# Experts' second half: conversions two half chunks ahead, sums behind the next quarter's first half chunk, the last group's work spread out

## The chip, the cores and the metric

The kernel runs on one core of a Trainium2 chip. The metric is the device time of one execution in microseconds (us), the median of several runs. The engines are TensorE (PE, with its weight loads PEld), VectorE (DVE), ScalarE (ACT), GpSimd (POOL) and SyncE (SP), whose queue here only issues DMAs. PE writes its results into eight PSUM banks of 128 x 512 fp32.

## What is computed

One layer for 512 tokens of width 2048: a mixer (pooling, retention, gates, an output projection) and behind it a PEER layer of 16384 experts. The change lies in the experts' second half and the end of the kernel. Cut to that, the reference is:

```
def block(args):                       # the experts, for 128 tokens
    xb, eb, gb = args                  # tokens, chosen experts, gates
    u = expert_u[eb]
    v = expert_v[eb]
    act = jax.nn.gelu(jnp.einsum('td,tkd->tk', xb, u))
    return jnp.einsum('tk,tkd->td', gb * act, v)
...
x = x + g2[:, None, :] * peer_ffn(fn, ...)
return rmsnorm(x, final_norm_gain)
```

## The kernel before, in words

Every fp32 product is made of three TensorE products: each operand is split into a high part (fp32r) and a low part, and `mm3` (lines 83 to 87) adds high x high, high x low and low x high. So each operand has to be converted: `split` (lines 71 to 74) has ACT write the high part (L73) and DVE the low part (L74).

**The first three blocks of 128 tokens** (`acc0` to `acc2`) are multiplied densely with all experts, **the fourth block** (`accg`) gathers its 128 chosen rows of `v` one after another: POOL issues an indirect DMA into one of three buffers `vrow` (L928), DVE multiplies the row by its coefficient and adds it to `accg` (L1078).

`experts_out` (L1052) runs over 16 groups of 8 x 128 experts. A group has four quarters of 512 output columns, and a quarter has four half chunks, so a group has 16 half chunks (the number `step` in the code, 0 to 15). A half chunk is 128 x 1024 values of `v`: two experts' 512 columns. For each, PE does 2 experts x 3 token blocks x 3 products = 18 matmuls (288 in a group), into three PSUM banks that the whole quarter adds up. `pairs` are the converted activations `ph` and `pl` that stand against it, eight per group.

What feeds PE in a group, in the order of the code:

- `half()` (L143) hands out a converted half chunk and then converts until `converted` of them are ready, here 1. A conversion takes 128 x 1024 of a 1 MB chunk `rawc` and writes `whc` (ACT) and `wlc` (DVE). There are three `whc`/`wlc` pairs and three `rawc` buffers; once both halves of a chunk are converted, `fill` issues the DMA for the third chunk after it on SP's queue. Half chunk s + 1 is thus converted in program order ahead of the matmuls of half chunk s.
- Behind the matmuls of half chunks 0, 1, 2, 4, 5, 6, 8, 10 and 12 one gathered row is added (L1078), until all 128 are done, which is early in the 15th group.
- At half chunk 4 `load_group` (L1032) issues the next group's gates `gt` and activations `at` on SP. At half chunks 9, 10, 11 and 13 `gate_in` has POOL multiply two of them by their gates (L1049), and `halves` has ACT and DVE convert them into `ph` and `pl`.
- At the end of a quarter DVE adds the three banks to `acc` (L1187). These sums stand in DVE's queue right behind the quarter's last half chunk, so DVE waits there until PE has finished it, and the conversion of the next quarter's second half chunk is queued behind them.

All engines work through their queues in program order (this part of the program is scheduled by hand).

**The last group** also ends the layer. `close(q)`, behind the second half chunk of a quarter, has POOL multiply that quarter of the four results by the row g2 (L1111), PE transpose the residual (L1115) and DVE add it (L1118). `finish` (L1121) multiplies the last banks by g2 (L1124), adds them (L1125) and has ACT sum the squares (L1105). The rows g2 and the final gain are loaded at the start of the stage, on ACT's queue (L1062, L1063). The last quarter goes block by block: its four half chunks are converted first (a fourth pair lies in `vrow`), then `close(3)` and `put` of the gathered block, then for each block 24 matmuls, `finish` and `put`. `put` (L1132) computes the inverse root mean square and scales two halves of 1024 columns: for three of the four tiles with two DVE instructions that multiply by the gain as well (L1139), for the last block with one on ACT (L1143) and one on DVE (L1141), after `gained` (L1130) has multiplied by the gain quarter by quarter, three times on POOL and in the last quarter on DVE.

## Time and profile before

| | us |
|---|---|
| median of 3 runs (5053.54 to 5059.59) | 5055.97 |
| the profiled execution's own time | 5052.76 |
| its span, first to last instruction | 5051.0 |
| PE busy in the span | 4850.2 (96%) |
| DVE / ACT / POOL busy in the span | 3240.8 / 1704.6 / 1504.5 |
| the experts' second half, from its first to its last matmul | 3890.04 to 5031.9 |

The profile is that of one execution. A busy share says little by itself here; what counts is where PE waits. The views used are: busy time per engine in stretches of time (with the granted clock of TensorE and the DMA engines' busy share), the list of who waited for whom, groups of instructions by line, and the instructions in order of time. Start times are from the start of the span. In an instruction's row the bracket says how long its engine stood idle before it and what ended that. Matmul ends are modelled: a matmul of 512 columns is drawn as 0.39 us but the next one starts about 0.227 us after it.

### The profile page before, as it was taken

The page shows a single profiled execution, that of the slowest core. Times are in us where ns is not written, and L with a number is a line of the kernel's source. Part 1 is how long each engine was busy: PE and PEld are TensorE (multiplying, and loading weights), DVE is VectorE, ACT ScalarE, POOL GpSimd, SP SyncE. Part 2 cuts the span into 40 slices and gives each one's busy share as a digit, 9 for nine tenths or more (in the row PEclk, how much of TensorE's full clock was granted, in tenths as well). Part 3 has the DMA queues.
Part 4 walks back from the last instruction along what each step waited for, and adds up shares of the span by engine and source line. Part 5 has one row for each costly group of instructions (what it writes and reads, how often), then busy time and mean ns, then how long its engine had stood idle before and what let it go on. Part 6 is the DMA issues. An engine that isn't in the chain of part 4 may idle for free.

```text
span 5051.0 us, 58652 instructions
## 1 busy us (share of the span) xinstructions
PE 4850.2 (96%) x22905; PEld 4181.8 (83%) x22905; DVE 3240.8 (64%) x4297; ACT 1704.6 (34%) x2700; POOL 1504.5 (30%) x1115
## 2 busy tenths in 40 slices
PE   6889999999999999999999999999999999999997
PEld 5668888888888888888778999999999777777776
DVE  8873333443432245565477998888786787887876
ACT  3232222222232222122232365556564322222222
POOL 6440000000000011000011478779685333333322
PEclk9999999999999999999999999999999999999999
DMA  6442233222233356665623688878888888888873
GB/s 261 177 144 94 94 102 102 94 100 101 93 135 122 123 215 241 233 243 204 214 91 107 222 285 296 300 273 304 307 303 315 292 312 302 289 298 296 308 250 134
DMA packets 268022, 1058.12 MB, mean 209 GB/s; under 512 B 22608, under 2 KB 73856, under 8 KB 172768
## 3 DMA queue, kind: packets, MB, share of 16 engines
q1 hardware_dynamic: 208240, 724.62, 41.6%
q0 software_dynamic: 54416, 325.48, 17.0%
q10 hardware_dynamic: 5088, 4.26, 0.3%
q8 instruction: 181, 2.97, 0.2%
q14 instruction: 97, 0.79, 0.0%
HBM read 973.53 MB, written 80.75 MB: 209 GB/s over the span
## 4 chain that ended last, share of the span: by engine, by line
PE 63%; DVE 14%; DMA 9%; issue 9%; POOL 2%; ACT 2%; SPq 1%; POOLq 0%; DVEq 0%; ACTq 0%
PE bank L86 21%; PE bank L87 20%; PE bank L85 20%; DMA at<-ga 4%; DVE wlc L74 3%; DMA rawc<-in_w_ada_dram 2%; DVE urow L977 2%; DMA gd<-gsc 1%; DVE rawc L187 1%; DMA rawc<-in_v_dram 1%; DVE accg L1078 1%; ACT whc L73 1%; DVE pl L74 1%; POOL ohx L917 1%; PE bank L906 1%
## 5 line engine op out<-in xcount | busy, mean ns | idle before, releaser
L74 DVE TENSOR_TENSOR wlc<-rawc,whc 128x1024 fp32r<-128x1024 f32 x904 | 1205.3, 1335 | 1018.3 <-ACT whc L73 1017.4
L73 ACT CAST whc<-rawc 128x1024 fp32r<-128x1024 f32 x967 | 999.5, 1050 | 2011.3 <-PE bank L86 1084.3
L85 PE MATMUL bank<-act,whc 128*128 128x512 f32 x2816 | 1102.5, 392 | 27.7 <-ACT act L346 19.8
L86 PE MATMUL bank<-act,whc 128*128 128x512 f32 x2816 | 1103.1, 392 | 23.6 <-DVE act L355 18.8
L87 PE MATMUL bank<-act,wlc 128*128 128x512 f32 x2816 | 1102.3, 391 | 6.7 <-POOL wlc L74 5.1
L87 PE MATMUL bank<-fh,wlc 128*128 128x384 f32 (+1 forms) x2304 | 791.9, 344 | 10.1 <-DVE wlc L74 8.9
L85 PE MATMUL bank<-fh,whc 128*128 128x384 f32 (+1 forms) x2304 | 793.0, 344 | 3.1 <-ACT fh L730 2.0
L86 PE MATMUL bank<-fl,whc 128*128 128x384 f32 (+1 forms) x2304 | 790.9, 343 | 0.6 <-DVE fl L733 0.5
L86 PE MATMUL bank<-wlc,ph 128*128 128x512 f32 x1530 | 607.5, 397 | 55.2 <-DVE wlc L74 55.2
L86 PEld LDWEIGHTS bank<-act,whc 128*128 128x128 f32 x2816 | 531.8, 189 | 140.5 <-DVE act L355 23.1
L85 PEld LDWEIGHTS bank<-act,whc 128*128 128x128 f32 x2816 | 532.2, 189 | 139.9 <-ACT act L346 19.8
L87 PEld LDWEIGHTS bank<-act,wlc 128*128 128x128 f32 x2816 | 531.9, 189 | 120.2 <-POOL wlc L74 6.6
L917 POOL TENSOR_SCALAR ohx<-iota,tr,gh 128x128 fp32r<-128x128 f32 x384 | 595.2, 1556 | 76.7 <-PE bank L906 72.6
L85 PE MATMUL bank<-whc,ph 128*128 128x512 f32 x1530 | 603.5, 394 | 4.6 <-ACT whc L73 3.1
L87 PE MATMUL bank<-whc,pl 128*128 128x512 f32 x1530 | 602.9, 394 | 0.0
L87 PEld LDWEIGHTS bank<-fh,wlc 128*128 128x128 f32 x2304 | 435.8, 189 | 22.5 <-DVE wlc L74 10.2
L85 PEld LDWEIGHTS bank<-fh,whc 128*128 128x128 f32 x2304 | 436.7, 190 | 13.4 <-ACT fh L730 2.3
L86 PEld LDWEIGHTS bank<-fl,whc 128*128 128x128 f32 x2304 | 436.0, 189 | 11.3 <-DVE fl L733 1.9
L86 PEld LDWEIGHTS bank<-wlc,ph 128*128 128x128 f32 x1530 | 291.7, 191 | 129.6 <-DVE wlc L74 69.4
L928 POOL DMA_INDIRECT vrow<-in_v_dram,eidx x128 | 222.5, 1738 | 519.6 <-DVE accg L1078 505.6
L187 DVE SCALAR_TENSOR_TENSOR rawc<-rawc,cond 128x2048 f32<-128x2048 f32 x96 | 239.8, 2498 | 182.3 <-DMA rawc<-in_w_ada_dram 182.2
L85 PEld LDWEIGHTS bank<-whc,ph 128*128 128x128 f32 x1530 | 291.6, 191 | 68.8 <-ACT whc L73 5.2
(289 smaller groups left out, 5236.4 us busy)
## 6 DMA issues: line engine op xcount, KB each, us to landing
rawc<-in_ut_dram SPq DMA_DIRECT2D x128, 1024.0 KB
rawc<-in_v_dram SPq DMA_DIRECT2D x128, 1024.0 KB
rawc<-in_w_ada_dram SPq DMA_DIRECT2D x96, 1024.0 KB
rawc<-in_w_v_dram SPq DMA_DIRECT2D x32, 1024.0 KB
rawc<-in_w_g_dram SPq DMA_DIRECT2D x32, 1024.0 KB
rawc<-in_w_br_dram SPq DMA_DIRECT2D x32, 1024.0 KB
ga<-gao SPq DMA_DIRECT2D x64, 384.0 KB
gd<-gsc SPq DMA_DIRECT2D x24, 1024.0 KB
```

The source lines that it names most:

```text
L73: nc.scalar.copy(out=h, in_=src)
L74: (eng or nc.vector).tensor_tensor(out=l, in0=src, in1=h.bitcast(FT), op=OP.subtract)
L85: mm(out, w[0], x[0], start=start, stop=False)
L86: mm(out, w[0], x[1], start=False, stop=False)
L87: mm(out, w[1], x[0], start=False, stop=stop)
L187: nc.vector.scalar_tensor_tensor(out=t, in0=t, scalar=1.0, in1=self.cond, op0=OP.mult, op1=OP.mult, accum_out=self.mod[:, j:j + 1])
L906: nc.tensor.matmul(bank[:, u * 2 * P:(u + 1) * 2 * P], y, x.rearrange("p h i -> p (h i)"), start=True, stop=True)
L917: nc.gpsimd.tensor_scalar(out=x[:, 0, :], in0=self.iota, scalar1=tr[:, 0, s], scalar2=gh[:, s].bitcast(FT), op0=OP.is_equal, op1=OP.mult)
L928: self.nc.gpsimd.indirect_dma_start(out=t, out_offset=None, in_=src, in_offset=bass.IndirectOffsetOnAxis(ap=self.eidx[:, k:k + 1], axis=0))
L977: nc.vector.scalar_tensor_tensor(out=u, in0=u, scalar=1.0, in1=fnat, op0=OP.mult, op1=OP.mult, accum_out=act[:, i:i + 1])
L1078: stt(out=accg, in0=v, scalar=c, in1=accg, op0=OP.mult, op1=OP.add)
```

## The change

In the 16 groups:

- `converted` becomes 2 and two more pairs (`w5`) are set up, five in all (`cycle` 5: three from the old buffers, two from the new). Half chunk s + 2 is now converted, in program order, ahead of the matmuls of half chunk s.
- The three sums of a quarter (`add_up`) move behind the first half chunk of the next quarter in the code, and so behind one more conversion.

In the last group and its neighbour:

- g2 and the gain are no longer loaded at the start of the stage. In the 15th group, at half chunk 13, SP issues the residual's first three parts, then g2 into the free `gt` buffer and the gain into the four free `at` buffers.
- `close` is split: `gate(q)` (POOL times g2) comes at half chunk 15 of the 15th group and at 2, 5, 8 of the last, `residual(q)` (transposes and additions) at 1, 4, 7, 10.
- `gained` is called for all four tiles and all quarters: 13 times on POOL, 3 times (last quarter) on DVE. `put` therefore scales each tile with one ACT and one DVE instruction.
- The conversions for the last quarter start at half chunks 10 and 11 (`converted` 3 and 4), all through the five pairs; `spare` goes. `put` of the gathered block comes before the last quarter's loop over blocks.

```diff
-        if self.extra_pair and self.pairs_made % 4 == 3:
+        if self.extra_pair and self.pairs_made % self.cycle >= 3:
             return self.extra_pair()
...
-            pp, ac, vp = tp("pp", 2), tp("ac"), tp("vp", 3)
+            pp, ac, vp, more = tp("pp", 2), tp("ac"), tp("vp", 3), tp("w5", 2)
+            self.extra_pair, self.cycle, self.converted = lambda: self.pair_of(more), 5, 2
...
-            nc.scalar.dma_start(out=g2, in_=self.g2row.to_broadcast([P, D]))
-            nc.scalar.dma_start(out=gain, in_=a["final_row"].to_broadcast([P, D]))
...
+            def load_lines():
+                g = self.gl.tile([P, ND // GC, G, GC], FT, name="gt").rearrange("p a b c -> p (a b c)")[:, :D]
+                nc.sync.dma_start(out=g, in_=self.g2row.to_broadcast([P, D]))
+                for q in range(4):
+                    w = self.ld.tile([P, 2, ND], FT, name="at").rearrange("p a b -> p (a b)")[:, :T]
+                    nc.sync.dma_start(out=w, in_=a["final_row"][:, cut(q)].to_broadcast([P, T]))
+                    lines[q] = g[:, cut(q)], w
...
+            def add_up(g, q, banks):
+                for t in range(NT):
+                    o = acc[t][:, cut(q)]
+                    if g == 0:
+                        nc.scalar.copy(out=o, in_=banks[t])
+                    else:
+                        tt(out=o, in0=o, in1=banks[t], op=OP.add)
...
+                    if last and step >= 10:
+                        self.converted = step - 7
+                    w = self.half()
+                    if hf == 0:
+                        banks = [self.bank() for _ in range(NT)]
...
+                    if full:
+                        add_up(*full)
+                        full = None
...
+                    if g == NGR - 2:
+                        if step == 13:
...
+                            for i in range(3):
+                                load(i)
+                            load_lines()
+                        if step == 15:
+                            gate(0)
+                    if last:
+                        if step in (2, 5, 8):
+                            gate(step // 3 + 1)
+                        if step in (1, 4, 7, 10):
+                            residual(step // 3)
...
+                            full = g, q, banks
...
             ws = [self.half() for _ in range(4)]
+            put(NT)
             for t in range(NT):
...
                 finish(t, 3, b)
                 put(t)
```

Three places where instructions stand in another order. The first is DVE's queue in the third quarter of a middle group: `wlc` is a conversion, `pl` the low part of an activation of the next group, `accg` a gathered row, `acc` a sum. Before, from the conversion of half chunk 10 to the first sum:

```order
L74 TENSOR_TENSOR wlc<-rawc,whc 128x1024
L74 TENSOR_TENSOR pl_32420<-at,ph_32419 128x384
L74 TENSOR_TENSOR pl_32424<-at,ph_32423 128x384
L74 TENSOR_TENSOR wlc<-rawc,whc 128x1024
L1078 SCALAR_TENSOR_TENSOR accg<-vrow,coef,accg 128x2048
L74 TENSOR_TENSOR pl_32457<-at,ph_32456 128x384
L74 TENSOR_TENSOR pl_32461<-at,ph_32460 128x384
L74 TENSOR_TENSOR wlc<-rawc,whc 128x1024
L74 TENSOR_TENSOR pl_32489<-at,ph_32488 128x384
L74 TENSOR_TENSOR pl_32493<-at,ph_32492 128x384
L1187 TENSOR_TENSOR acc_30221<-acc_30221,bank 128x512
```

And the same place now, from the conversion of half chunk 11 to the first sum:

```order
L74 TENSOR_TENSOR wlc<-rawc,whc 128x1024
L74 TENSOR_TENSOR pl_33833<-at,ph_33832 128x384
L74 TENSOR_TENSOR pl_33837<-at,ph_33836 128x384
L74 TENSOR_TENSOR wlc<-rawc,whc 128x1024
L1076 SCALAR_TENSOR_TENSOR accg<-vrow,coef,accg 128x2048
L74 TENSOR_TENSOR pl_33868<-at,ph_33867 128x384
L74 TENSOR_TENSOR pl_33872<-at,ph_33871 128x384
L74 TENSOR_TENSOR wlc<-rawc,whc 128x1024
L74 TENSOR_TENSOR pl_33902<-at,ph_33901 128x384
L74 TENSOR_TENSOR pl_33906<-at,ph_33905 128x384
L74 TENSOR_TENSOR wlc<-rawc,whc 128x1024
L1160 TENSOR_TENSOR acc_30224<-acc_30224,bank 128x512
```

The rows stand in nearly the same sequence, but each `wlc` now belongs to the half chunk after the one it belonged to (11, 12, 13 where it was 10, 11, 12), and one more, for half chunk 14, stands ahead of the sums.

The second is POOL's queue in the last group, with the multiplications by g2 (`rows` before, `gt` now) and by the gain (`rows` and `at`). Before, between the first and the second quarter's gates, and now:

```order
L1130 TENSOR_TENSOR acc_30223<-acc_30223,rows 128x512
L1111 TENSOR_TENSOR acc_30221<-acc_30221,rows 128x512
L1111 TENSOR_TENSOR acc_30222<-acc_30222,rows 128x512
L1111 TENSOR_TENSOR acc_30223<-acc_30223,rows 128x512
L1111 TENSOR_TENSOR accg<-accg,rows 128x512
```

```order
L1140 TENSOR_TENSOR accg<-accg,at 128x512
L1117 TENSOR_TENSOR acc_30224<-acc_30224,gt 128x512
L1117 TENSOR_TENSOR acc_30225<-acc_30225,gt 128x512
L1117 TENSOR_TENSOR acc_30226<-acc_30226,gt 128x512
L1117 TENSOR_TENSOR accg<-accg,gt 128x512
L1140 TENSOR_TENSOR acc_30224<-acc_30224,at 128x512
L1140 TENSOR_TENSOR acc_30225<-acc_30225,at 128x512
L1140 TENSOR_TENSOR acc_30226<-acc_30226,at 128x512
L1140 TENSOR_TENSOR accg<-accg,at 128x512
```

A quarter now has four multiplications by the gain on POOL where it had one.

The third is DVE's queue at the very end, from the scaling of the second block to the sum of squares of the third, before and now:

```order
L1139 SCALAR_TENSOR_TENSOR acc_30222<-acc_30222,rt1r,rows 128x1024 x2
L1124 TENSOR_TENSOR last<-bank,rows 128x512
L1125 TENSOR_TENSOR acc_30223<-acc_30223,last 128x512
L1130 TENSOR_TENSOR acc_30223<-acc_30223,rows 128x512
L1134 TENSOR_REDUCE s_37886<-ssq 128x1
```

```order
L1149 TENSOR_SCALAR acc_30225<-acc_30225,rt1r 128x1024
L1133 TENSOR_TENSOR last<-bank,gt 128x512
L1134 TENSOR_TENSOR acc_30226<-acc_30226,last 128x512
L1140 TENSOR_TENSOR acc_30226<-acc_30226,at 128x512
L1144 TENSOR_REDUCE s_37909<-ssq 128x1
```

Two instructions of 1024 columns became one; the other half of the scaling went to ACT.

## Rows read from the trace of the kernel before

**Rows 1.** Busy time by stretch: length; PE, PEld, DVE, ACT, POOL; clock; DMA share; GB/s.

```profile
3890.04:3965.25 75.21, 69.50 (x288) 55.98 (x289) 51.98 (x41) 28.79 (x42) 22.88 (x17) 0.95 0.92 342
...
4107.01:4177.69 70.68, 67.39 (x289) 55.01 (x288) 56.73 (x46) 20.37 (x24) 24.10 (x17) 0.98 0.83 297
...
4884.18:4949.46 65.28, 65.28 (x289) 54.05 (x288) 43.97 (x39) 21.67 (x26) 18.36 (x12) 1.00 0.63 204
4949.46:5031.74 82.28, 75.74 (x353) 60.06 (x351) 52.03 (x70) 23.89 (x44) 25.66 (x15) 1.00 0.31 107
...
3965.25:4884.18 918.93, 872.33 (x3745) 712.10 (x3744) 736.39 (x584) 266.42 (x315) 307.21 (x220) 0.98 0.83 296
```

**Rows 2.** Who PE waited for in groups 1 to 13: us, times, longest.

```profile
PE bank L86 <- DVE wlc L74: 46.6, 26, 2.3
```

**Rows 3.** Instructions in order of time, third quarter of group 3: DVE, POOL, PE.

```profile
4140.45 1.22 DVE L74 TENSOR_TENSOR wlc<-rawc,whc 128x1024 fp32r<-128x1024 f32 x1
...
4148.45 4.79 DVE L74 TENSOR_TENSOR wlc<-rawc,whc 128x1024 fp32r<-128x1024 f32 x1 [0.39 <-ACT whc L73]
...
4156.36 3.53 DVE L74 TENSOR_TENSOR wlc<-rawc,whc 128x1024 fp32r<-128x1024 f32 x1
4159.81 1.01 DVE L74 TENSOR_TENSOR pl<-at,ph 128x384 fp32r<-128x384 f32 x2
...
4148.21 3.94 POOL L1049 TENSOR_TENSOR at<-at,gt 128x384 f32<-128x384 f32 x4
...
4159.94 0.79 PE L86 MATMUL bank<-wlc,ph 128*128 128x512 f32 x1 [2.27 <-DVE wlc L74]
4160.53 0.63 PE L87 MATMUL bank<-whc,pl 128*128 128x512 f32 x1
4160.96 0.63 PE L85 MATMUL bank<-whc,ph 128*128 128x512 f32 x1
```

**Rows 4.** DVE's instructions of group 3 by line: busy us, mean ns, idle before.

```profile
L74 DVE TENSOR_TENSOR wlc<-rawc,whc 128x1024 fp32r<-128x1024 f32 x16 | 25.4, 1588 | 2.0 <-ACT whc L73 2.0
L1078 DVE SCALAR_TENSOR_TENSOR accg<-vrow,coef,accg 128x2048 f32<-128x2048 f32 x9 | 21.1, 2345 | 0.0
L1187 DVE TENSOR_TENSOR acc<-acc,bank 128x512 f32<-128x512 f32 x13 | 8.7, 685 | 10.4 <-PE bank L87 10.4
L74 DVE TENSOR_TENSOR pl<-at,ph 128x384 fp32r<-128x384 f32 x8 | 4.4, 582 | 1.6 <-ACT ph L73 1.6
```

**Rows 5.** Group 3 in order of time: SP's issue of the gates, POOL's first use.

```profile
4125.80 0.63 SPq L1038 DMA_DIRECT2D gt<-gd  x1
...
4144.73 2.19 POOL L1049 TENSOR_TENSOR at<-at,gt 128x384 f32<-128x384 f32 x2 [8.37 <-DMA at<-ga]
```

**Rows 6.** Group 0 in order of time: the load of g2, a chunk's issue, its first use.

```profile
3888.57 0.33 ACTq L1062 DMA_DIRECT2D rows<-g2row  x1
...
3892.64 0.37 SPq L106 DMA_DIRECT2D rawc<-in_v_dram  x1
...
3913.83 2.00 ACT L73 CAST whc<-rawc 128x1024 fp32r<-128x1024 f32 x2 [5.44 <-DMA rawc<-in_v_dram]
```

**Rows 7.** The last group by line: POOL's multiplications by g2, PE's transposes.

```profile
L1111 POOL TENSOR_TENSOR acc<-acc,rows 128x512 f32<-128x512 f32 x9 | 18.2, 2050 | 0.0
L1111 POOL TENSOR_TENSOR accg<-accg,rows 128x512 f32<-128x512 f32 x3 | 3.8, 1281 | 0.0
...
L1115 PE MATMUL bank<-ident,vrow 128*128 128x128 f32 x64 | 7.6, 272 | 0.0
```

**Rows 8.** The end in order of time: PE's last matmul, DVE's last two blocks.

```profile
5031.51 0.40 PE L87 MATMUL bank<-vrow,pl 128*128 128x512 f32 x1
...
5033.59 0.69 DVE L1124 TENSOR_TENSOR last<-bank,rows 128x512 f32<-128x512 f32 x1
...
5039.83 0.68 DVE L1124 TENSOR_TENSOR last<-bank,rows 128x512 f32<-128x512 f32 x1
...
5044.28 0.75 DVE L1141 TENSOR_SCALAR acc<-acc,rt2r 128x1024 f32<-128x1024 f32 x1
```

More of the change, by code (lines that the diff above doesn't have):

```diff
@@ L1053, in experts_out @@
         nc, a, tc = self.nc, self.a, self.tc
[L1054 removed]
+        NT, NGR = ND // P, P // G
         with ExitStack() as cs:
             tp = lambda n, b=1: cs.enter_context(tc.tile_pool(name=n, bufs=b, reuse_waits="tile"))
[L1057 removed]
+            pp, ac, vp, more = tp("pp", 2), tp("ac"), tp("vp", 3), tp("w5", 2)
+            self.extra_pair, self.cycle, self.converted = lambda: self.pair_of(more), 5, 2
             acc = [ac.tile([P, D], FT, name=f"acc{t}") for t in range(NT)]
             accg = ac.tile([P, D], FT, name="accg")
[L1060 to L1063 removed]
             stt, tt = nc.vector.scalar_tensor_tensor, nc.vector.tensor_tensor
@@ L1105, in squares, with gate, residual @@
                 nc.scalar.activation(out=j, in_=tiles[t][:, cut(q)], func=AF.Square, accum_out=ss[:, t, q:q + 1])
-            def close(q):
+            def gate(q):
                 for t in range(TT):
                     o = tiles[t][:, cut(q)]
-                    nc.gpsimd.tensor_tensor(out=o, in0=o, in1=g2[:, cut(q)], op=OP.mult)
+                    nc.gpsimd.tensor_tensor(out=o, in0=o, in1=lines[q][0], op=OP.mult)
+            def residual(q):
                 for t in range(TT):
@@ L1119, in close @@
                 squares(NT, q)
+                gained(NT, q, nc.gpsimd)
             def finish(t, q, bank):
                 o = acc[t][:, cut(q)]
-                m = ac.tile([P, T], FT, name="last", bufs=2)
-                tt(out=m, in0=bank, in1=g2[:, cut(q)], op=OP.mult)
+                m = ac.tile([P, T], FT, name="last")
+                tt(out=m, in0=bank, in1=lines[q][0], op=OP.mult)
                 tt(out=o, in0=o, in1=m, op=OP.add)
                 squares(t, q)
+                gained(t, q, nc.vector if q == 3 else nc.gpsimd)
             def gained(t, q, eng):
                 o = tiles[t][:, cut(q)]
-                eng.tensor_tensor(out=o, in0=o, in1=gain[:, cut(q)], op=OP.mult)
+                eng.tensor_tensor(out=o, in0=o, in1=lines[q][1], op=OP.mult)
             def put(t):
@@ L1137, in put @@
                     o = tiles[t][:, half]
-                    if t != NT - 1:
-                        stt(out=o, in0=o, scalar=r, in1=gain[:, half], op0=OP.mult, op1=OP.mult)
-                    elif i:
+                    if i:
                         nc.vector.tensor_scalar(out=o, in0=o, scalar1=r, scalar2=None, op0=OP.mult)
@@ new lines, in experts_out @@
+            full = None
+            for g in range(NGR):
+                last = g == NGR - 1
+                for step in range(12 if last else 16):
+                    q, hf = step // 4, step % 4
+                    if last and step >= 10:
[3 more added lines that the diff above has]
+                        banks = [self.bank() for _ in range(NT)]
+                    for u in (0, 1):
+                        h, l = pairs[g * G + 2 * hf + u]
+                        s = slice(u * T, (u + 1) * T)
+                        for t in range(NT):
+                            ts = slice(t * P, (t + 1) * P)
+                            self.mm3(banks[t], (h[:, ts], l[:, ts]), (w[0][:, s], w[1][:, s]),
+                                     hf + u == 0, hf == 3 and u == 1)
+                    if full:
+                        add_up(*full)
+                        full = None
+                    if step == 4:
+                        self.load_group()
+                    if len(pairs) < (g + 1) * G:
+                        halves(2)
+                    if step in (0, 1, 2, 4, 5, 6, 8, 10, 12):
+                        next(rows, None)
+                    if step in (9, 10, 11, 13):
+                        self.gate_in(2)
+                        halves(2)
+                    if g == NGR - 2:
+                        if step == 13:
@@ L1177, in experts_out @@
                                 load(i)
-                        if last and hf == 1:
-                            close(q)
-                            if q == 0:
-                                load(3)
-                    for t in range(NT):
-                        o = acc[t][:, cut(q)]
-                        if g == 0:
-                            nc.scalar.copy(out=o, in_=banks[t])
-                        elif not last:
-                            tt(out=o, in0=o, in1=banks[t], op=OP.add)
-                        else:
-                            finish(t, q, banks[t])
-                    if last:
-                        gained(NT - 1, q, nc.gpsimd)
-            def spare():
-                t = vp.tile([P, D], FR, name="vrow")
-                return t[:, :D // 2], t[:, D // 2:]
-            self.extra_pair, self.converted = spare, 2
+                            load_lines()
[6 more added lines that the diff above has]
+                            residual(step // 3)
+                            if step == 1:
+                                load(3)
+                    if hf == 3:
+                        if last:
+                            for t in range(NT):
+                                finish(t, q, banks[t])
+                        else:
+                            full = g, q, banks
             ws = [self.half() for _ in range(4)]
+            put(NT)
             for t in range(NT):
-                if t == 0:
-                    close(3)
-                    put(NT)
                 b = self.bank()
```

34 lines of the change are left out of this document (2 added, 32 removed).

## The prediction, made before the changed kernel had run

> **What bounds the kernel now.** I read the stretches first, one per group of 288 matmuls [rows 1]. Group 14 is the yardstick: 65.28 us, PE busy for all of it, clock 1.00, and no wait of PE anywhere in it. That is 0.227 us a matmul, 4.08 us a half chunk. It is also the group in which hardly any gathered rows are left for DVE: 43.97 us of work, against 56.73 in group 3. Group 3 takes 70.68 us, and groups 1 to 13 together 918.93 where 13 times 65.28 would be 848.64: 70.3 us too long. PE's waits [rows 2] name the cause of 46.6 of them: 26 waits, two in each group, all for the low part `wlc`, written by DVE. [...]
>
> Then I read one such place [rows 3]. The conversion of half chunk 11, which takes 1.22 us elsewhere, takes 4.79: four POOL multiplications started 0.24 us ahead of it, and it ends 1.1 us after their run. That of 12 takes 3.53 and ends at 4159.89; PE's matmul follows at 4159.94 after 2.27 us of idleness. DVE is not short of time in a group: 25.4 + 21.1 + 8.7 + 4.4 = 59.6 us, blocking included and slightly overlapping in the trace, is under 65.28 [rows 4]. It is late at one place, since a conversion is only one half chunk (4.08 us) ahead there.
>
> **The change, groups 1 to 13.** No instruction is added here. The order decides: what was the conversion of 11, 12 in DVE's queue is now that of 12, 13, and that of 14 follows, ahead of the sums. I keep the times of [rows 3] and only rename. Group 3 starts at 4107.01, so an unhindered PE begins half chunk 12 at 4107.01 + 12 x 4.08 = 4155.97, half chunk 13 at 4160.05, and 14 at 4164.13. Conversion 12, in the place of the 4.79 us, ends at 4148.45 + 4.79 = 4153.24, 2.7 us early. Conversion 13 ends at 4159.89, 0.2 us early. Conversion 14 comes behind two `pl` (4159.81 + 1.01) and 1.22 us: 4162.0, 2.1 us early. Even with POOL's blocking as it was, no wait is left, though one place is tight.
>
> It gets looser by the gates. SP's issue of `gt` waits in its queue behind the chunk that the conversion of half chunk 5 frees. Before, it went at 4125.80, 18.8 us into the group [rows 5]. Now DVE, starting the group with three sums, three rows and the conversions of 3, 4 and 5 (3 x 0.685 + 3 x 2.345 + 3 x 1.22 = 12.8 us, rates from [rows 3, 4]), frees it some 6 us sooner. POOL's first multiplication waited 8.37 us for that data [rows 5], so it and all behind it moves up by as much as the code allows. The sums behind the next half chunk cost PE nothing: three banks more are in use for 4 us, of eight. The quarter as a whole fits too: three sums, two rows, four conversions and six `pl` are 2.1 + 4.7 + 4.9 + 3.5 = 15.2 us, and 5.9 us of blocking (16 x (1.588 - 1.22), [rows 3, 4]) makes 21.1 against 16.3 of PE; the 4.8 us too many are less than the 8.2 us by which conversions now lead, and the next quarter (three sums, one row, four conversions, two `pl`: 10.5 us) gives them back. I take 0.3 us a group as left over for the tight place: **a gain of 66 us**, between 53 (a wait of 0.7 us and its slow matmuls, 0.6, stay in each) and 70.
>
> The DMA engines must carry a group in less time: 0.83 x 70.68 = 58.7 us of work per group [rows 1], 0.90 of 65.28. That still fits, with cover for conversions that come late.
>
> **Group 0.** 75.21 us, 9.9 too many [rows 1]. At its start ACT's queue loads g2 and gain, 1 MB each; a chunk issued at 3892.64 was first used at 3913.83, after ACT had waited 5.44 us for it [rows 6]. These 2 MB (5.6 us at 342 / 0.92 = 372 GB/s, the rate of fully busy DMA engines there) move 1000 us later. With that and the greater lead I take **7 us**; the first `ph`, for which PE waits at the start, stays, and chunks may still land late. Bounds 3 and 8.4.
>
> **Group 14.** 65.28 has nothing to give. The new loads there (2 MB beside the residual's 3) fall into a stretch where the DMA engines are 0.63 busy [rows 1]. g2 is queued behind a chunk and three residual parts: 5 MB at that rate, 14 us from about half chunk 13, lands about 2 us into the last group (half chunks 13 to 15 are 12 us), and `gate(0)` needs 4 x 2.05 us [rows 7], so it ends about when the first residual's transposes do (2 x 4.08 + 7.6 / 4, [rows 7]). I book 0; if g2 came 6 us later, the queue behind the additions would cost PE about that once.
>
> **The last group.** 82.28 us, with 64 transposes, 7.6 us, that stay: 65.28 + 7.6 leaves 9.4 too many [rows 1, 7]. The split of `close` lets PE run on while POOL multiplies. POOL gets ten multiplications more, 1.28 us each when undisturbed [rows 7], 13 us in a group where it is busy for 25.66 of 82 [rows 1]. [...] I leave 3 us: **a gain of 6.4**, between 2 and 9.
>
> [...]
>
> **The tail.** PE's last matmul ends at 5031.91, but DVE turns to the last block only at 5039.83 [rows 8]: 7.9 us of DVE lagging. Its blocks were 5039.83 - 5033.59 = 6.24 us apart, while PE needs 24 x 0.227 = 5.44. The last block already had the form that now all have (gain separately, scaling halved between ACT and DVE): from 5039.83 to 5044.28 + 0.75 = 5.2 us of DVE. So DVE keeps up, and the lag left is what `finish` of the third quarter and the gathered block's `put` push into it: six instructions of 0.69 and some 2.4 us (an estimate: the 5.2 us less two additions, the gain and the wait for the squares ahead of it), against 5.44 until the first block is ready, after conversions that may end a little late: 1.5 to 3.3 us. **A gain of 5.4**, between 3 and 7.9. What follows the last `finish`, 11.2 us to the end of the span, is unchanged.
>
> **Sum.** 66 + 7 + 0 + 6.4 + 5.4 = 84.8 us; 5052.8 - 84.8 = 4968 for the profiled execution, whose time is 3.2 us under the median of the runs; so **4971 us**. With all upper bounds, 70 + 8.4 + 9 + 7.9 = 95.3: 4961. With all lower ones, 53 + 3 + 2 + 3 = 61: 4995. What I count as no change is less than 0.2% (10 us), about what a measurement of this kernel can tell.
>
> **Rivals.** (a) *DVE stays late in the third quarter.* If POOL, which now has its data earlier and more in one piece, blocks DVE for longer runs (DVE loses 3.9 instead of the 2.3 us behind 12), conversion 13 comes 1.4 us late in each group. Against it: the gates' data comes earlier, so that the lead absorbs it. Price: 13 x 1.4 us of waiting, times 70.3 / 46.6 for the clock behind it, is 27 us, and some 5 us more in the last group: about 5003 us (4995 to 5035). Chance 0.14.
>
> (b) *The lead doesn't come about.* ACT and DVE are in-order; if the two new pairs are not free when asked (their space waits for old users) or the sums, which wait for PE, hold everything behind them, DVE is as late as before: 5046 to 5062. Against it: in [rows 4] DVE idles 10.4 us a group waiting for PE's banks, and time to run ahead is just what the pairs open. Chance 0.04.
>
> (c) *Slower: the ring of three chunks becomes the bound.* A chunk's DMA is issued when the conversion of half chunk n is done, and its own first conversion is n + 5. If every chunk took as long as the one of [rows 6], 21.2 us, a half chunk could not come faster than 21.2 / 5 = 4.24 us: 67.8 a group, still a gain. From 22.1 us on (70.7 x 5 / 16) it is a loss; at 23 us a group takes 73.6, 2.9 us more in 14 groups: about 5097. For it: DMA work fills 0.90 of the time. Against it: 21.2 us was the worst case, with 2 MB more on the way, and in groups 1 to 13 PE's waits name DVE alone. Chance 0.04.
>
> The forecast (4957 to 4995) has 0.78. The range reaches from just under the likeliest case's bound into (a): 4957 to 5002. Faster by over 0.2%: 0.78 + 0.14 + 0.01 = 0.93; within: 0.03; slower: 0.04.
>
> **What would show it.** Right: groups 1 to 13 at 65.3 to 66 us, clock 1.00, PE's list without `wlc`; `gt` issued some 13 us into a group; ACT waiting for PE's banks no more at each conversion; PE's last matmul to the last `finish` under 3.5 us. Wrong: conversions of 3 us and more with PE waiting at half chunk 13 (a); ACT or DVE idle before `rawc` or `vrow` DMAs in every group (c); PE idle in the last group behind `gate`.

## The result and the profile after

| | before | after | ratio, 95% interval |
|---|---|---|---|
| median of 4 runs each | 5055.91 us | 4983.14 us (4974.80 to 4986.13) | 0.9853, 0.9836 to 0.987 |

The change makes the kernel 1.5% faster: 72.8 us. The forecast was 4971 us, a gain of 85; 4983 lies inside the range. The profiled execution after took 4985.34 us, span 4983.6.

Busy time by stretch of the kernel after, with the columns of [rows 1]; the stretches are group 0, 3, 14, the last group, and groups 1 to 13:

```profile
3904.43:3971.18 66.75, 66.28 (x288) 54.02 (x289) 53.17 (x44) 30.08 (x44) 24.87 (x17) 1.00 0.97 356
4102.68:4168.44 65.76, 65.76 (x289) 54.06 (x288) 55.64 (x46) 20.14 (x24) 31.53 (x17) 1.00 0.87 311
4825.93:4891.70 65.77, 65.77 (x289) 54.06 (x288) 36.42 (x39) 21.63 (x26) 9.80 (x8) 1.00 0.65 219
4891.70:4966.00 74.30, 73.19 (x353) 60.60 (x351) 53.36 (x62) 22.84 (x43) 49.48 (x29) 1.00 0.33 116
3971.18:4825.93 854.75, 854.75 (x3745) 702.83 (x3744) 737.05 (x583) 264.12 (x315) 361.06 (x220) 1.00 0.89 320
```

In groups 1 to 13 PE is busy for 854.75 of 854.75 us and the granted clock is 1.00; before it was 918.93 us at 0.98 [rows 1]. Over the whole second half, PE's waits (us in total, times, longest) are down to

```profile
PE bank L86 <- DVE wlc L74: 1.6, 2, 1.1
PE bank L85 <- ACT ph L73: 1.0, 1, 1.0
```

against 26 waits of 46.6 us in groups 1 to 13 alone [rows 2]. What the stage gave, term by term, from the two profiles (the last group ends with PE's last matmul, the tail runs from there to the end of the span):

| us | before | after | gain | forecast |
|---|---|---|---|---|
| group 0 | 75.21 | 66.76 | 8.45 | 7 |
| groups 1 to 13 | 918.93 | 854.75 | 64.18 | 66 |
| group 14 | 65.28 | 65.77 | -0.49 | 0 |
| last group | 82.44 | 74.47 | 7.97 | 6.4 |
| tail | 19.09 | 17.42 | 1.67 | 5.4 |
| sum, from the stage's first matmul | 1160.95 | 1079.1 | 81.8 | 84.8 |
| start of the stage | 3890.04 | 3904.43 | -14.4 | none |
| span | 5051.0 | 4983.6 | 67.4 | 84.8 |

Two things stand out: the stage itself gave nearly what was forecast, and the stage started 14.4 us later, in code that the change doesn't touch. The experiments ask what the lead and the late sums are worth apart, why a group takes 65.77 and not 65.28 us, where the tail's gain stayed, and what the late start is.

### The profile page after: what moved, and what is told of

It is laid out like the page before. It is cut to its first block, busy times and chain, and to the rows that moved or that the text cites. A ratio compares the mean times of both kernels' runs of the same rounds, so it can differ in the third digit from the quotient of the medians.

```text
span 4983.6 us, 58696 instructions
## 1 busy us (share of the span) xinstructions
PE 4832.4 (97%) x22905; PEld 4173.4 (84%) x22905; DVE 3237.4 (65%) x4296; ACT 1704.9 (34%) x2703; POOL 1570.5 (32%) x1125
## 4 chain that ended last, share of the span: by engine, by line
PE 72%; DVE 11%; issue 8%; DMA 5%; POOL 2%; ACT 2%; SPq 0%; POOLq 0%; DVEq 0%; ACTq 0%
PE bank L87 24%; PE bank L85 24%; PE bank L86 24%; DVE wlc L74 2%; DVE urow L978 1%; DVE rawc L188 1%; DMA gd<-gsc 1%; DMA rawc<-in_w_ada_dram 1%; POOL ohx L918 1%; DVE u L513 1%; DMA x<-m 1%; ACT whc L73 1%; PE bank L907 1%; DVE gsc L898 0%; DVE eq L869 0%
## 5 line engine op out<-in xcount | busy, mean ns | idle before, releaser
L74 DVE TENSOR_TENSOR wlc<-rawc,whc 128x1024 fp32r<-128x1024 f32 x905 | 1158.3, 1286 | 993.5 <-ACT whc L73 992.9
L929 POOL DMA_INDIRECT vrow<-in_v_dram,eidx x128 | 273.7, 2138 | 488.4 <-DVE accg L1076 473.2
L87 PEld LDWEIGHTS bank<-whc,pl 128*128 128x128 f32 x1536 | 288.2, 188 | 64.8 <-DVE pl L74 0.3
```

What stands on the lines that cost most here:

```text
L74: (eng or nc.vector).tensor_tensor(out=l, in0=src, in1=h.bitcast(FT), op=OP.subtract)
L87: mm(out, w[1], x[0], start=False, stop=stop)
L929: self.nc.gpsimd.indirect_dma_start(out=t, out_offset=None, in_=src, in_offset=bass.IndirectOffsetOnAxis(ap=self.eidx[:, k:k + 1], axis=0))
```

## Experiment 1: the lead and the late sums, apart

The changed kernel once more, and three with one or both parts undone. The lead back to one half chunk (all five pairs stay):

```diff
-            self.extra_pair, self.cycle, self.converted = lambda: self.pair_of(more), 5, 2
+            self.extra_pair, self.cycle, self.converted = lambda: self.pair_of(more), 5, 1
```

The sums back to the end of the quarter:

```diff
-                            full = g, q, banks
+                            add_up(g, q, banks)
```

Nothing undone:

> The changed kernel once more, nothing edited. In the changed kernel's profile the experts' second half started 14.4 us later than in the profile of before (3904.43 against 3890.04 us), with the instructions and buffers ahead of it unchanged. If that is scatter between executions, this run starts the second half anywhere between some 3885 and 3910 us, and its own length, first to last matmul, stays at 1061 us within 1. If something in the change lengthens the stages ahead, it starts at 3904 again within 3 us. Time: 4970 to 4986 us in the first case, 4983 in the second.

The lead undone:

> The changed kernel with conversions one half chunk ahead again in the groups (five pairs kept, the sums still behind the next quarter's first half chunk, the last group as changed). If the second half chunk of lead is what removed the waits: they come back at half chunks 11 and 12, though shorter than before, since the conversion behind the sums no longer waits for them; about 1 to 2 us a group, with the slower clock behind them, groups 1 to 13 at 67 to 69 us, and 20 to 40 us more than the changed kernel. If the place of the sums is what counted: groups stay under 66 us and the time is that of the changed kernel within 5 us.

The sums undone:

> The changed kernel with the sums at the end of their quarter again, conversions two half chunks ahead. If the lead alone suffices: groups 1 to 13 at 65.8 us and no wait of PE in them, time as the changed kernel within 5 us. If the place of the sums is needed: DVE, which waits for PE's banks before it may convert, is 4 us later behind each quarter's end and the tight conversion (of half chunk 13, 0.2 us early by the forecast) comes late: waits of 1 to 2 us a group, 66.5 to 69 us a group, 10 to 40 us more.

Both undone; the work in the last group stays spread out:

> The changed kernel with both undone, conversions one ahead and sums at the end of their quarter; what stays is the last group's spread, the later loads and two pairs more. If the forecast's sums are right, groups 1 to 13 are back at 70.7 us and only the terms of group 0 (part of 8.5 us), the last group (8) and the tail (2) are left: 5030 to 5045 us. If the five pairs alone help (ACT no longer waits for PE's release of a pair), groups come out at 67 to 69 us and the time at 5000 to 5020.

Measured, with ratios to the kernel before in the same runs:

| | median us | ratio, 95% interval | group 0 | groups 1 to 13 | last group | tail |
|---|---|---|---|---|---|---|
| changed kernel again | 4973.14 | 0.9839, 0.9823 to 0.9856 | 67.06 | 854.75 | 74.47 | 17.4 |
| lead 1, late sums | 5018.65 | 0.9935, 0.9918 to 0.9952 | 71.37 | 885.18 | 84.63 | 14.6 |
| lead 2, sums at the end | 4975.88 | 0.9841, 0.9825 to 0.9858 | 66.67 | 854.75 | 74.47 | 17.1 |
| lead 1, sums at the end | 5055.76 | 1.0002, 0.9993 to 1.0012 | 71.24 | 921.81 | 84.04 | 14.3 |

Groups 1 to 13 (columns of [rows 1]) and PE's waits in them, first with lead 1 and late sums, then with neither:

```profile
3967.07:4852.25 885.18, 863.34 (x3746) 705.14 (x3745) 745.98 (x583) 267.04 (x316) 363.29 (x219) 0.99 0.86 308
...
PE bank L86 <- DVE wlc L74: 21.8, 14, 2.3
```

```profile
3973.31:4895.12 921.81, 878.02 (x3746) 712.41 (x3745) 736.71 (x584) 267.79 (x317) 322.24 (x220) 0.98 0.84 295
...
PE bank L86 <- DVE wlc L74: 43.8, 26, 2.3
```

The lead alone removes every wait: with the sums at the quarter's end PE is again busy for all of groups 1 to 13:

```profile
3965.24:4819.99 854.75, 854.75 (x3746) 702.83 (x3745) 734.77 (x584) 265.51 (x316) 333.58 (x220) 1.00 0.89 319
```

The late sums alone remove one of the two waits of a group, mostly that at half chunk 11 (14 left of 26), and take 36.6 of the 67 us; the expectation had both waits staying, shorter. The kernel is 45.5 us slower than the changed one in the same runs (20 to 40 expected). Together they give no more than the lead. What is left with neither of them (the loads moved, the last group spread out) can't be told from no change: the 4.0 us in group 0 and the 3.2 in last group and tail stand against 2.9 more in groups 1 to 13, where experiment 3 shows a cost of the new pairs. So the expected 5030 to 5045 us didn't come, though the groups came out as expected (70.9 us each). What failed is the gain of 8 us in the last group: with the work spread out as in the changed kernel but a lead of one, it takes 84.04 and 84.63 us, more than the 82.44 before. That gain hangs on the lead. Whether the spreading adds to it beside the lead wasn't tried. Group 0 splits as well: without the lead it takes 71.24 us, so 4.0 of its 8.45 us come without it (g2 and gain are no longer loaded there, and there are five pairs) and 4.5 from it.

The changed kernel's second profile started the stage at 3905.57 us, within 3 us of the first, which is what the theory of a lengthening by the change had. Experiment 5 comes back to this.

## Experiment 2: POOL's gate multiplications as the cause of the late conversions

The kernel before, without POOL's multiplication by the gates, and with nothing else changed:

```diff
-            self.nc.gpsimd.tensor_tensor(out=zv, in0=zv, in1=gt, op=OP.mult)
```

> The kernel before without POOL's multiplication of the experts' activations by their gates (8 of 128 x 384 in a group); the result is therefore not the layer's. If POOL's runs of multiplications, which stretch DVE's conversions at half chunks 11 and 12 from 1.22 to 4.8 and 3.5 us, are what makes PE wait: no conversion takes over 1.3 us there, PE waits under 0.5 us a group and groups 1 to 13 take 65.3 to 66 us each, with conversions only one half chunk ahead. If DVE's own load in that quarter (rows, low parts, sums) is the cause: waits of 1 to 2 us stay at half chunks 11 and 12 and groups take 67 to 69 us.

One run, 4991.47 us, of a kernel whose output isn't the layer's. Conversions in group 3 by line, as in [rows 4], and groups 1 to 13:

```profile
L74 DVE TENSOR_TENSOR wlc<-rawc,whc 128x1024 fp32r<-128x1024 f32 x16 | 19.6, 1223 | 4.0 <-ACT whc L73 4.0
```

```profile
3970.73:4822.86 852.13, 851.17 (x3745) 702.02 (x3744) 657.63 (x584) 262.54 (x315) 204.39 (x116) 1.00 0.89 319
```

All sixteen conversions take 1.22 us on average, where it was 1.59 [rows 4], and with a lead of one half chunk and the sums in their old place groups 1 to 13 lose 66.8 us. So POOL's multiplications caused the waits, all but 3.5 us, which are left at half chunk 12 (0.1 to 0.7 us in most groups). The run takes two things away at once, the stretching of the conversions, and the wait of ACT and DVE for POOL's product ahead of `ph` and `pl`; it doesn't tell how much each of them cost. The change doesn't remove POOL's multiplications but makes room for them.

## Experiment 3: why a group takes 65.77 us

Half chunks 4 to 7 of group 3 after, one per row (columns of [rows 1]):

```profile
4119.09:4123.23 4.14, 4.14 (x20) 3.38 (x18) 4.14 (x4) 1.05 (x1) 0.72 (x1) 1.00 1.05 399
4123.23:4127.35 4.12, 4.12 (x20) 3.38 (x19) 4.12 (x4) 1.05 (x1) 2.40 (x2) 1.00 1.20 297
4127.35:4131.48 4.13, 4.13 (x20) 3.38 (x18) 3.96 (x3) 1.05 (x1) 2.41 (x2) 1.00 1.06 408
4131.48:4135.56 4.08, 4.08 (x20) 3.38 (x19) 1.16 (x2) 1.05 (x1) 0.64 (x1) 1.00 1.02 407
```

PE waits for nothing and the clock is 1.00, yet three half chunks take 0.04 to 0.06 us too long. The pattern repeats every five half chunks, the cycle of the pairs: the first two slow ones stream from the new pairs, which lie at bytes 184768 to 201152 of a partition, the third follows them. It is the same in group 14, where hardly any gathered rows are left. So I moved the new pairs to another place, next to the old ones (73600 to 89984), by the order in which the pools are opened, and then to the middle (122752 to 139136):

```diff
-            pp, ac, vp, more = tp("pp", 2), tp("ac"), tp("vp", 3), tp("w5", 2)
+            more, pp, ac, vp = tp("w5", 2), tp("pp", 2), tp("ac"), tp("vp", 3)
```

```diff
-            pp, ac, vp, more = tp("pp", 2), tp("ac"), tp("vp", 3), tp("w5", 2)
+            pp, more, ac, vp = tp("pp", 2), tp("w5", 2), tp("ac"), tp("vp", 3)
```

> The changed kernel with the two new pairs set up first instead of last in the stage: they lie at bytes 73600 to 90000 of a partition instead of 184768 to 201000, and the buffers of the gathered rows lie at 176576 and up; no instruction is added or moved. In the changed kernel every group without a wait takes 65.77 us instead of 65.28: of every five half chunks the two with operands in the new pairs and the one after them take 4.12 to 4.14 us, the other two 4.08. If TensorE reads operands more slowly from the higher addresses, all half chunks take 4.08 and groups 1 to 13 take 848.6 us instead of 854.75, the stage 7 us less. If it is the alternation between two sets of buffers, or five pairs in use, the pattern and the 854.75 stay.

> The changed kernel with its two new pairs in the middle of the buffers (122752 to 139136 bytes in a partition; 184768 to 201152 in the changed kernel, 73600 to 89984 where they were moved down), all else as in the changed kernel. Theory 1 (only buffers near the top slow the matmuls that stream from them): groups 1 to 13 take 848.6 us, 65.28 each, as with the low place. Theory 2 (the matmul's pace falls gradually with the address): between, 850.5 to 852 us, 65.4 to 65.5 a group. Theory 3 (all places but those next to the first three pairs are slow, or it is the neighbours acc and vrow in use by other engines that matter): 854.7 us, 65.75 a group.

Groups 1 to 13, low place and then middle:

```profile
3956.80:4805.44 848.64, 848.64 (x3746) 702.70 (x3745) 733.25 (x583) 264.78 (x315) 376.86 (x220) 1.00 0.90 322
```

```profile
3964.28:4812.92 848.64, 848.64 (x3746) 702.94 (x3744) 736.82 (x583) 264.27 (x315) 369.99 (x220) 1.00 0.90 322
```

Both give 65.28 us in each of the 13 groups: the pace of group 14 before, with no wait. The order of the buffers is the cause, and by the pattern it is the place of the new pairs (buffers set up behind them move up by 16384 bytes as well). It is not a gradual matter of the address, since the middle is as good as the low place.

The kernel before shows the same. In its last quarter the fourth pair lies in a `vrow` buffer, at bytes 178624 to 186816. The first of each six matmuls, from the end of its second block through the third (six from `vrow`, then six from each of three low pairs, then `vrow` again):

```profile
5024.83 0.40 PE L85 MATMUL bank<-vrow,ph 128*128 128x512 f32 x1
...
5026.22 0.40 PE L85 MATMUL bank<-whc,ph 128*128 128x512 f32 x1
...
5027.61 0.40 PE L85 MATMUL bank<-whc,ph 128*128 128x512 f32 x1
...
5028.99 0.39 PE L85 MATMUL bank<-whc,ph 128*128 128x512 f32 x1
...
5030.35 0.40 PE L85 MATMUL bank<-vrow,ph 128*128 128x512 f32 x1
```

Six from `vrow` take 1.39 us, the six behind them 1.39, then 1.38 and 1.36, the usual pace. What it is about the high place, and why the matmuls behind are slow too, stays open. The low place took 4964.93 us (0.9822, 0.9807 to 0.9838); its stage is 7.6 us shorter than the changed kernel's (1071.55 against 1079.1), which says more than the medians (experiment 5). The middle place, in one run, took 4971.98.

## Experiment 4: what keeps the tail long

The end of the kernel after. First DVE in order of time: conversions of the last half chunks, `finish` of the third quarter, `put` of the gathered block (its first instruction, and one of 1 column), the first instruction of the last quarter's first and last block. Then PE's last matmul:

```profile
4950.38 2.62 DVE L74 TENSOR_TENSOR wlc<-rawc,whc 128x1024 fp32r<-128x1024 f32 x2 [1.79 <-ACT whc L73]
4952.93 0.68 DVE L1133 TENSOR_TENSOR last<-bank,gt 128x512 f32<-128x512 f32 x1
...
4955.52 1.55 DVE L1134 TENSOR_TENSOR acc<-acc,last 128x512 f32<-128x512 f32 x1
...
4958.51 0.15 DVE L1144 TENSOR_REDUCE s<-ssq 128x1 f32<-128x4 f32 x1
...
4959.73 1.28 DVE L246 TENSOR_TENSOR rt3t<-rt3r 128x1 f32<-128x1 f32 x1
...
4962.37 0.68 DVE L1133 TENSOR_TENSOR last<-bank,gt 128x512 f32<-128x512 f32 x1
...
4973.02 0.68 DVE L1133 TENSOR_TENSOR last<-bank,gt 128x512 f32<-128x512 f32 x1
...
4965.79 0.39 PE L87 MATMUL bank<-whc,pl 128*128 128x512 f32 x1
```

PE ends at 4966.18, and its first block of the last quarter was done two blocks of 5.53 us earlier, at 4955.1 (at the slower pace of experiment 3). DVE comes to it at 4962.37, 7.3 us late, and nearly keeps that: 5.3 us a block, and 6.84 us late at the last.

**Gates earlier.** If POOL's late set of multiplications holds up DVE, the three later sets can each come three half chunks sooner: two sets at half chunk 15 of the 15th group, then one each at 2 and 5 of the last:

```diff
                         if step == 15:
                             gate(0)
+                            gate(1)
                     if last:
-                        if step in (2, 5, 8):
-                            gate(step // 3 + 1)
+                        if step in (2, 5):
+                            gate(step // 3 + 2)
```

> The changed kernel with the last group's multiplications by g2 one quarter earlier on POOL: two quarters at the end of the 15th group, then one at half chunks 2 and 5, none at 8. In the changed kernel DVE takes up the first block of the last quarter at 4962.4, 7 us after PE has finished it, since POOL's fourth set (4938.4 to 4947.4) and four conversions hold each other up. If that is the cause of the tail's lag: DVE's last block starts 1 to 3 us behind PE's last matmul instead of 7, the single wait of PE at half chunk 10 (1.11 us) is gone, and the end comes 5 to 7 us earlier. If the lag is DVE's own work (three blocks of 5.2 us and what stands ahead of them), it stays within 1 us.

The same with the new pairs in the low place:

> Both of the above. If both causes are right, first matmul of the stage to the end of the span takes 1065 to 1068 us instead of 1079, and the time is 4960 to 4972 us, with the scatter of the stages ahead of it (some 15 us) on top; if neither is, 1079 and the changed kernel's time.

The first took 4977.33 us (0.9841, 0.9825 to 0.9857), the second 4968.67 (0.9828, 0.9814 to 0.9842). Last group and tail together took 89.99 us where the changed kernel has 91.89, and 89.13 where the low place alone has 90.98: 1.9 us each, and in the medians nothing that can be told. DVE's last block starts 5.0 us behind PE's last matmul (6.84 before this edit): neither the 1 to 3 us of the one theory nor the other's no change. PE's wait of 1.1 us at half chunk 10, which the expectation had going away, stayed, so POOL's multiplications by g2 aren't its cause. Both together took 1070.7 us from the stage's first matmul, not the 1065 to 1068 hoped for. DVE in the first of them, conversions at the end:

```profile
4936.89 5.13 DVE L74 TENSOR_TENSOR wlc<-rawc,whc 128x1024 fp32r<-128x1024 f32 x4 [1.79 <-ACT whc L73]
...
4947.64 2.61 DVE L74 TENSOR_TENSOR wlc<-rawc,whc 128x1024 fp32r<-128x1024 f32 x2 [1.79 <-ACT whc L73]
```

Four conversions now take 5.13 us, nearly undisturbed. But the last two can't start sooner: DVE waits 1.79 us for ACT's half of the conversion, which stands in ACT's queue behind the squares of the gathered block, and these need DVE's sums behind PE's transposes at half chunk 10. The chain ahead of the last conversions goes through three engines, and POOL was only a part of it.

**`put` of the gathered block out of the way**, in the kernel with the low place: its chain stands behind the first block's squares, where DVE waits anyhow (0.85 to 1.13 us a block), and ACT scales both halves:

```diff
                 squares(t, q)
+                if q == 3 and t == 0:
+                    put(NT)
                 gained(t, q, nc.vector if q == 3 else nc.gpsimd)
...
-                    if i:
+                    if i and t < NT:
                         nc.vector.tensor_scalar(out=o, in0=o, scalar1=r, scalar2=None, op0=OP.mult)
...
             ws = [self.half() for _ in range(4)]
-            put(NT)
```

> The kernel with the pairs moved down, and the put of the gathered block taken out of DVE's way at the end: its chain is issued in the first block's finish, where DVE waits for ACT's squares anyhow (0.85 to 1.13 us a block), and its scaling goes wholly to ACT. Theory (the lag at the end is the DVE work that stands ahead of the last quarter's first block): DVE's way loses the wait of 1.1 us, one scaling of 0.76 and the 1.1 us by which POOL holds one small instruction of the chain: from PE's last matmul to the last finish 6.1 becomes 3 to 3.6 us, the stage to the end of the span 1071.6 becomes 1068.6 to 1069.2. Rival (the lag is set elsewhere, by ACT's squares or POOL's gain multiplications ahead of each block): 5.5 to 6.1 us remain, stage 1071 to 1071.6. In the median 3 us is less than can be told: 4958 to 4968, ratio 0.981 to 0.983 to before.

4964.95 us (0.9822, 0.9806 to 0.9839). PE's last matmul ended at 4942.17. DVE in its last quarter, the first block's start, the same small instruction, the wait for the first block's root, and the last block's start:

```profile
4933.94 0.69 DVE L1133 TENSOR_TENSOR last<-bank,gt 128x512 f32<-128x512 f32 x1
...
4936.68 0.16 DVE L246 TENSOR_TENSOR rt3t<-rt3r 128x1 f32<-128x1 f32 x1
...
4939.82 0.16 DVE L245 RECIPROCAL rt0r<-rt0t 128x1 f32<-128x1 f32 x1 [1.55 <-ACT rt0t L244]
...
4946.72 0.68 DVE L1133 TENSOR_TENSOR last<-bank,gt 128x512 f32<-128x512 f32 x1
```

The lag is 4.55 us instead of 6.1 with the low place alone. DVE's work came out of the way, but half of it came back as a wait: ACT, with both halves of the gathered block to scale, delivers the first block's root 1.55 us late. Neither the theory (3 to 3.6) nor the rival (5.5 to 6.1) has the number right; part of the lag is DVE's work, and taking it off DVE costs where ACT is next.

## Experiment 5: the late start

The kernel before, profiled once more:

> The kernel before, unchanged, profiled once more, to see whether the start of the experts' second half (3890.0 us in the first profile of before, 3895.7 to 3905.6 in the kernels with the change or parts of it at the same addresses, 3890.2 with the pairs moved down) differs between executions or between kernels. Theory 1 (scatter between executions; instructions and addresses ahead of the stage are the same): somewhere between 3890 and 3906, most likely above 3893. Theory 2 (something of the change makes the earlier part slower): 3889.5 to 3891, as before. The stage itself by both: 1161 us within 1, group 0 75.2, groups 1 to 13 919 within 1.

The first matmul of the second half, in the two profiles of the kernel before (3890.04 in the first) and in the profile after:

```profile
3899.43 0.50 PE L85 MATMUL bank<-whc,ph 128*128 128x512 f32 x1 [1.60 <-ACT ph L73]
```

```profile
3904.43 0.50 PE L85 MATMUL bank<-whc,ph 128*128 128x512 f32 x1 [0.98 <-ACT ph L73]
```

The same kernel starts its second half 9.4 us apart in two executions, and the stage then takes 1160.3 us, 0.7 less than the first time. Over the thirteen profiles of all kernels the start lies between 3887.2 and 3905.6: 3895.7 to 3905.6 in the six with the new pairs in the high place, 3887.2 to 3901.1 in the seven others. Instructions and addresses ahead of the stage are the same before and after. So the start differs by 9.4 us with no change at all; whether the change adds the rest of the 14.4 us isn't told by so few (the means of the two sets are 3901.4 and 3894.7). Part of the difference is PE's waits in the experts' first half, between 2840 and 3600 us (20.6 us in the first profile before, 22.7 in the second, 29.6 after). The rest wasn't taken apart, and why the starts differ from one execution to the next was not found.

For a comparison of kernels this means that the stage, from its first matmul, is the sharper measure: 1079.1 and 1079.4 us in two profiles of the changed kernel, whose medians lie 10 us apart (4983.14 and 4973.14). The second of these medians is 2 us from the forecast, the first 12.

## Why the prediction was right, and where it was not

**The lead: right, with more room than worked out.** Group 3 after, each engine in order of time: SP's issue of the gates, POOL's multiplications, and DVE's conversions for half chunks 12, 13 and 14:

```profile
4114.21 0.50 SPq L1039 DMA_DIRECT2D gt<-gd  x1
...
4142.83 3.95 POOL L1050 TENSOR_TENSOR at<-at,gt 128x384 f32<-128x384 f32 x4
...
4151.47 2.00 POOL L1050 TENSOR_TENSOR at<-at,gt 128x384 f32<-128x384 f32 x2
...
4145.42 2.45 DVE L74 TENSOR_TENSOR wlc<-rawc,whc 128x1024 fp32r<-128x1024 f32 x1 [2.74 <-ACT whc L73]
...
4150.99 3.56 DVE L74 TENSOR_TENSOR wlc<-rawc,whc 128x1024 fp32r<-128x1024 f32 x1
...
4155.42 1.21 DVE L74 TENSOR_TENSOR wlc<-rawc,whc 128x1024 fp32r<-128x1024 f32 x1
```

The half chunks begin at 4152.02, 4156.10 and 4160.18, so the conversions end 4.1, 1.6 and 3.6 us early; renaming [rows 3] gave 2.7, 0.2 and 2.1. Of the 1.4 us more, 0.4 are PE, which comes later by its slower matmuls. The other 1.0 goes with the gates, issued 11.5 us into the group (18.8 before; some 13 forecast): POOL's run of four starts 40.2 us into the group instead of 41.2. Rival (a) named a real thing, a conversion of 3.56 us at the tight place, which was 1.6 us early all the same. Rivals (b) and (c) didn't come about; the DMA engines' share rose to 0.89 as forecast, and in groups 1 to 13 PE waits for nothing. Only in group 0 did ACT still wait for chunks (5.16 us for one), and PE lost 0.5 us there at half chunk 13.

**The 0.3 us a group left over: wrong in kind.** Nothing of the old waits was left. The 64.2 us are 70.3 (all that there was) less 13 x 0.47 us of slower matmuls, a term which the prediction didn't have: it took the pace of [rows 1] as a property of the matmuls, wherever their operands lie. That the sum came within 2 us of 66 is chance. The lower bound's 0.6 us for the slow matmuls behind a wait was the author's estimate. In [rows 3] the matmuls behind the wait start 0.43 us apart instead of 0.227. Before, PE was busy 23.7 us longer than 848.64 over 26 waits, at a clock of 0.98 [rows 1, 2]: 0.9 us a wait. With lead 1 and late sums it was busy 8.6 us longer than 854.75 over 14 waits, at 0.99: 0.6 us a wait (experiment 1). There 21.8 us of waiting cost 30.4 in all, 1.4 times as much; the factor in rival (a)'s price, 70.3 / 46.6, is 1.5.

**ACT's waits for PE's banks: the sign named for them was wrong.** ACT's conversions in group 3, by line, after:

```profile
L73 ACT CAST whc<-rawc 128x1024 fp32r<-128x1024 f32 x16 | 16.7, 1050 | 34.2 <-PE bank L87 22.8 <-DVE acc L1160 6.1 <-DVE wlc L74 3.1
```

It still waits 22.8 us for PE (28.3 before). With the lead filled, a pair comes free only when PE has used it, so such a wait now tells that ACT is ahead.

**POOL against DVE.** The prediction kept POOL's blocking as [rows 3] has it, a conversion that waited out a run of four. The rows after show the like: in group 3 the conversion at 4150.99 outlasts POOL's two multiplications from 4151.47 by 1.08 us, though it started first. In the last group, three conversions and three multiplications by g2 side by side take

```profile
4921.26 5.98 DVE L74 TENSOR_TENSOR wlc<-rawc,whc 128x1024 fp32r<-128x1024 f32 x3 [1.79 <-ACT whc L73]
```

```profile
4921.62 6.75 POOL L1117 TENSOR_TENSOR acc<-acc,gt 128x512 f32<-128x512 f32 x3
```

2.0 and 2.25 us each, where they take 1.22 and 1.28 alone. No wait was left in groups 1 to 13, and one of 1.1 us in the last. In groups 1 to 13 it is the lead that made it so, since the long conversions are still there; in the last group the 1.1 us stayed when the multiplications by g2 were moved (experiment 4). The 3 us that the forecast left in the last group were the author's estimate, and no run shows them: the group took 74.47 us, 1.6 more than 65.28 + 7.6 [rows 1, 7], of which 1.1 are that wait.

**Group 0 and the last group: right in size, the second for another reason.** They gave 8.45 us, at its upper bound of 8.4, and 7.97, inside its bounds. For the last group the prediction named the split of `close`, which lets PE run on while POOL multiplies. With the split and a lead of one the group takes 84.0 to 84.6 us (experiment 1), so the gain comes with the lead. The g2 that `gate(0)` needs was no trouble: POOL began with it 2.2 us into the group (about 2 forecast), and no wait of PE stands behind it.

**The tail: mis-sized, 1.7 instead of 5.4 us.** The step that failed is "1.5 to 3.3 us" for the lag. It took DVE as free when the third quarter's banks are, or a little later; PE finished these at 4949.6 us. The last conversions ended at 4952.93, 3.35 us later; the six instructions of `finish` took 5.6 us instead of 4.1, since some of them take longer beside POOL's gain multiplications (one 1.55 us, the same instruction for the block ahead 0.69); and the `put` took 3.9 instead of 2.4, with 1.28 us for an instruction on one column. That is 3.35 + 5.58 + 3.86 less the 5.53 us of PE's first block: 7.3 us of lag at the first block and 6.84 at the last, where it was 7.9. So the lag gave 1.1 us; the other 0.6 are what follows the last `finish`, 10.6 us where the prediction had 11.2 unchanged. Beneath it lies that last group and tail are not two terms. PE got 8.0 us faster in the last group, while DVE's work there didn't get less (52.03 us busy before, 53.36 after). With a lead of one, PE is 10 us slower in the last group and DVE's lag at the last block is 4.0 instead of 6.84 us: part of what PE saves turns into lag.

**The carry to the median.** The start of the stage was taken as fixed. It differed by 9.4 us between two executions of the kernel before, and one profile of each kernel, with 3.2 us added, can't say better than that. So 4983 against 4971 us is no test of the mechanism; the stage's 81.8 against 84.8 us is the better one, and part of that agreement is luck, as said of groups 1 to 13 and the last group.

## To carry to other kernels

Where an in-order engine is late at one place only, and not short of time on the whole, one or two more buffers ahead of it can take the whole loss, its slow matmuls included (here two more pairs took 46.6 us of waits and 23.7 us of longer matmuls out of groups 1 to 13); look first at how early each item would be with the old times renamed. When a faster engine runs ahead of the one that finishes the work, write the end as one sum for both, since part of what the first saves turns into lag of the second (here 4.0 us of lag with a lead of one and 6.84 with two). And after a move of buffers, compare the pace of matmuls that wait for nothing (here 4.08 against 4.12 to 4.14 us a half chunk).

## What was not expected of the hardware

- The pace of matmuls differed with the place of the operand that they stream: 4.12 to 4.14 us for a half chunk from bytes 184768 to 201152, and 4.13 for the one behind, against 4.08 for the others in the profile after; 65.28 us a group in the two runs with the pairs from 73600 or 122752, against 65.77. It costs 6.1 us in groups 1 to 13. No wait stands there and the granted clock is 1.00. The kernel before has it too where it streams from `vrow` (1.39 us for six matmuls, against 1.36).
- Beside POOL's `at` x `gt` multiplications a DVE conversion took 2.45 and 3.56 us in group 3 after and 4.79 in [rows 3] (1.22 alone), and ended 1.1 us after POOL's run each time, whichever had started first; beside `acc` x g2 multiplications conversions took 2.0 us each. Why the two differ was not tried.
- An instruction on a single column (L246) took 1.28 us in the profile after for the gathered block, beside POOL's gain multiplications, and 0.16 for the other three, when POOL had none left.
